# Attention scores: the rounding-remainder pass split into two 64-row matmuls on different keys

## The chip, the cores and the metric

The kernel runs on one NeuronCore of a Trainium2 chip. The metric is the device time of one execution in microseconds (us). TensorE (PE) multiplies, VectorE (DVE), ScalarE (ACT) and GpSimd (POOL) do the elementwise work, SyncE (SP) and others issue the transfers. A change is called faster or slower when it moves the time by more than 0.3%, 7.9 us here.

## The reference, cut to what matters

Two layers of a diffusion backbone. The part that is touched is the differential attention of the first layer: six heads, each with two sets of queries and keys of 64 channels and one set of values of 128 channels; 1024 latent tokens ask, 256 context tokens and the 1024 latent tokens answer.

```python
s = jnp.einsum('bqhcd,bkhcd->bchqk', qi, k) * scale      # c = 0, 1: two score maps per head
p = jax.nn.softmax(s, axis=-1)
wgt = p[:, 0] - lam * p[:, 1]
return jnp.einsum('bhqk,bkhe->bqhe', wgt, v)
```

## The kernel before, in words

Everything is computed in fp32. A matmul operand is kept as two rounded parts, high and low (fp32r), and a product of two operands is the sum of products of the parts. `spill_q` and `spill_k` (L661 to L673) leave the queries and keys of each head in DRAM, transposed, with both parts: `qt_d[h, c, part, 64 channels, token]` and `kt_d[h, c, copy, 64 channels, part, key]`, where the two copies of the keys are equal.

`head_load` (L840) brings one head into SBUF. The tile `q` has on its 128 partitions the high part of the 64 channels and below it the low part; the tile `k` has the same 64 channels of the keys on both halves, once with the high and once with the low part. So a matmul over 128 rows gives (query high + query low) times one part of the keys, and `s_mm` (L856) makes the scores of 128 queries against 1280 keys in six matmuls: three stretches of keys (512, 512, 256 columns, one PSUM bank each), each with the high and then the low part of the keys.

`attention` (L780) walks over 48 tiles of 128 queries (6 heads of 8 tiles), software pipelined. Its order is written by hand and pinned on PE, ACT, DVE and POOL: each of these engines works through its instructions in the order of the program. In one step s the order is

- PE: `s_mm` for c=0; transposes `wT` group 0 of tile s-2; `s_mm` for c=1; (every second step two transposes of `pair_out`); 4 matmuls of `pv`; `wT` group 1; 6 matmuls of `pv`; `wT` group 2.
- DVE: `combine` of tile s-1 (a reciprocal and a scalar product, L883 and L884, which need the row sums of the exponential for c=1 of the last step); the two row maxima for c=0 (L867); their minimum after negation (L871); (a copy of `pair_out`, L928); the two maxima for c=1; an operation of the head's tail (`tail_op`, L938 to L950) if there is one; the minimum for c=1 (L871); the copy L909 of `wT` group 2.
- ACT: the copy L907 of `wT` group 0; the exponential for c=0 (L877); (two squares of `pair_out`, L931); the copy L907 of group 1; the exponential for c=1.
- POOL: the two operations of `combine` of tile s-1, L889 (scale) and L890 (add), on 128x1280 elements; then what `head_load` issues, one part per step.

The score tile `s` has two buffers of three PSUM banks, one for c=0 and one for c=1, so `s_mm` for c waits until the exponential for c of the last step has read them. The tile of the transposes, `tr`, has one buffer: `wT` group 1 waits for the copy of what stands there before, group 2 for the copy L907 of group 1.

`head_load` of head h+1 runs during head h: a transfer for `q` in the second step, for `k` (c=0 and c=1) in the third and fourth, all three issued by POOL, and one for `v` issued by SP in the fifth. The transfers of the first head are issued in the stage before.

Of the kernel before, what the change touches and what calls it, by code (L numbers as in the profile page):

```python
# [10 lines left out]
F32R = mybir.dt.float32r  # L11
# [6 lines left out]
P = 128  # L18
D = 1024
SEQ = 1024  # L20
CTX = 256
NK = SEQ + CTX
# [4 lines left out]
NT = SEQ // P  # L27
# [19 lines left out]
class Net:  # L47
# [791 lines left out]

    def head_load(self, h, hp, hd):  # L840
        nc = self.nc
        qs = hp.tile([P, 2, SEQ], F32R, tag="q", name=self.name("q"))
        ks = hp.tile([P, 2, 2, NK], F32R, tag="k", name=self.name("k"))
        v = hp.tile([P, NK], F32, tag="v", name=self.name("v"))
        hd[h] = {"q": qs, "k": ks, "v": v, "o": self.xt([P, NT, P]),
                 "z0": self.small([P, NT], "z0", 2), "ms": self.small([P, NT], "ms", 2)}
        yield
        nc.gpsimd.dma_start(out=qs, in_=self.qt_d[h].rearrange("c a p t -> (a p) c t"))
        yield
        for c in range(2):  # L850
            nc.gpsimd.dma_start(out=ks[:, c], in_=self.kt_d[h, c].rearrange("d p a t -> (d p) a t"))
            yield
        nc.sync.dma_start(out=v, in_=self.v_d[h])
        yield

    def s_mm(self, st, c):  # L856
        nc, hd, t = self.nc, st["h"], st["t"]
        st["s"][c] = s = self.sp.tile([P, NK], F32, tag="s", name=self.name("sc"))
        for o0, n in ((0, 512), (512, 512), (1024, 256)):
            for a in range(2):  # L860
                nc.tensor.matmul(s[:, o0:o0 + n], hd["q"][:, c, t * P:(t + 1) * P], hd["k"][:, c, a, o0:o0 + n],  # L861
                                 start=(a == 0), stop=(a == 1))
        st["nm"][c] = self.small([P, 2], "nm")

    def s_max(self, st, c, i):
# [827 lines left out]
```

## Time and profile before

| | |
|---|---|
| time before, median of 3 runs | 2635.67 us (2633.87 to 2640.92) |
| the profiled execution: time | 2635.35 us |
| the profiled execution: span from first to last instruction | 2633.6 us |
| mean granted TensorE clock | 0.989 of full |
| PE busy | 2539.0 us (96%) |
| DVE busy | 1849.5 us (70%) |
| ACT busy | 1255.7 us (48%) |
| POOL busy | 949.5 us (36%) |
| score matmuls (L861) | 576, first start 341.2 us, last 654.2 us |

Busy is the sum of the durations that the profile shows for an engine, as a share of the span. Matmuls are pipelined: the next one starts before the end that is shown for the last. The score matmuls mark the attention stage, some 313 us of the span.

### The profile page before, as it was taken

The page shows a single profiled execution, that of the slowest core. Times are in us where ns is not written, and L with a number is a line of the kernel's source. Part 1 is how long each engine was busy: PE and PEld are TensorE (multiplying, and loading weights), DVE is VectorE, ACT ScalarE, POOL GpSimd, SP SyncE. Part 2 cuts the span into 40 slices and gives each one's busy share as a digit, 9 for nine tenths or more (in the row PEclk, how much of TensorE's full clock was granted, in tenths as well). Part 3 has the DMA queues.
Part 4 walks back from the last instruction along what each step waited for, and adds up shares of the span by engine and source line. Part 5 has one row for each costly group of instructions (what it writes and reads, how often), then busy time and mean ns, then how long its engine had stood idle before and what let it go on. Part 6 is the DMA issues. An engine that isn't in the chain of part 4 may idle for free. (4 is left out here: it accounts for less than half of the span.)

```text
span 2633.6 us, 33489 instructions
## 1 busy us (share of the span) xinstructions
PE 2539.0 (96%) x12251; PEld 2111.1 (80%) x12251; DVE 1849.5 (70%) x2862; ACT 1255.7 (48%) x2363; POOL 949.5 (36%) x582
## 2 busy tenths in 40 slices
PE   6999989999988999999999999999999999999999
PEld 5999977777777888888888877888888788888887
DVE  4777678888777555579877665666788655668884
ACT  5332356666343333358775323553654333338780
POOL 5432356666013223125461211230424232205452
PEclk8999999999999999999999999999999999999999
DMA  9577532320532333543303375447123333463302
GB/s 272 178 235 238 188 118 67 103 95 1 212 133 83 107 117 110 186 169 127 128 33 132 121 255 176 136 136 267 66 98 102 105 112 112 136 248 128 114 28 91
DMA packets 206290, 359.84 MB, mean 137 GB/s; under 512 B 16455, under 2 KB 110490, under 8 KB 201006
## 3 DMA queue, kind: packets, MB, share of 16 engines
q1 hardware_dynamic: 180816, 270.10, 31.5%
q0 software_dynamic: 10144, 47.19, 5.3%
q10 hardware_dynamic: 15166, 40.42, 4.0%
q8 instruction: 96, 1.57, 0.2%
q14 instruction: 68, 0.56, 0.1%
HBM read 264.56 MB, written 93.10 MB: 136 GB/s over the span
## 5 line engine op out<-in xcount | busy, mean ns | idle before, releaser
L105 DVE TENSOR_TENSOR w<-s,w 128x512 fp32r<-128x512 f32 (+3 forms) x311 | 291.6, 954 | 199.7 <-ACT w L104 196.9
L130 PE MATMUL ps<-w,hid 128*128 128x512 f32 x928 | 362.4, 390 | 2.4 <-DVE x L1347 2.3
L132 PE MATMUL ps<-w,hid 128*128 128x512 f32 x928 | 361.1, 389 | 0.0
L131 PE MATMUL ps<-w,hid 128*128 128x512 f32 x928 | 361.1, 389 | 0.0
L104 ACT CAST w<-s 128x512 fp32r<-128x512 f32 (+2 forms) x313 | 212.9, 693 | 296.6 <-POOL s L1151 76.7
L112 ACT CAST tr<-h 128x512 fp32r<-128x512 f32 x392 | 220.7, 587 | 109.1 <-DVE w L113 50.5
L1285 POOL TENSOR_TENSOR h<-h,h 128x2048 f32<-128x2048 f32 x36 | 170.6, 4743 | 141.1 <-DVE h L1253 92.5
L1151 POOL TENSOR_TENSOR s<-s,s 128x512 f32<-128x512 f32 x36 | 48.3, 1343 | 440.2 <-DVE w L105 440.2
L130 PEld LDWEIGHTS ps<-w,hid 128*128 128x128 f32 x928 | 174.2, 188 | 40.3 <-issue 2.8
L132 PEld LDWEIGHTS ps<-w,hid 128*128 128x128 f32 x928 | 174.2, 188 | 36.1
L131 PEld LDWEIGHTS ps<-w,hid 128*128 128x128 f32 x928 | 174.2, 188 | 35.6
L877 ACT ACTIVATE e<-sc,nm 128x1280 f32<-128x1280 f32 x96 | 127.6, 1329 | 106.6 <-DVE nm L871 104.9
L113 DVE TENSOR_TENSOR hid<-h,tr 128x512 fp32r<-128x512 f32 x196 | 132.0, 685 | 54.3 <-ACT tr L112 51.2
L1288 POOL TENSOR_TENSOR h<-h,h 128x2048 f32<-128x2048 f32 x14 | 70.7, 5053 | 264.6 <-DVE h L1285 264.6
L130 PE MATMUL ps<-h,w 128*128 128x512 f32 x416 | 165.0, 397 | 0.1
L131 PE MATMUL ps<-h,w 128*128 128x512 f32 x416 | 162.8, 391 | 1.4 <-DVE h L296 1.4
L132 PE MATMUL ps<-h,w 128*128 128x512 f32 x416 | 163.0, 392 | 0.0
L861 PE MATMUL sc<-k,q 128*128 128x512 f32 (+1 forms) x576 | 139.9, 380 | 14.0 <-ACT e L877 12.2
L867 DVE TENSOR_REDUCE nm<-sc 128x1 f32<-128x768 f32 x192 | 148.6, 816 | 0.4 <-PE sc L861 0.4
L890 POOL TENSOR_TENSOR e<-e,e 128x1280 f32<-128x1280 f32 x47 | 136.3, 2901 | 3.9
L861 PEld LDWEIGHTS sc<-k,q 128*128 128x128 f32 x576 | 103.7, 193 | 40.7 <-ACT e L877 20.1
L114 ACT CAST hid<-h 128x512 fp32r<-128x512 f32 x196 | 119.4, 623 | 23.7 <-PE ps L131 15.5
(325 smaller groups left out, 6600.0 us busy)
## 6 DMA issues: line engine op xcount, KB each, us to landing
s<-in_ffn_w_dram SPq DMA_DIRECT2D x80, 512.0 KB
hid_d<-h SPq DMA_DIRECT2D x28, 1024.0 KB
h<-hid_d SPq DMA_DIRECT2D x56, 512.0 KB
ad<-in_ada_w_dram SPq DMA_DIRECT2D x48, 512.0 KB
h<-in_ffn_w_dram SPq DMA_DIRECT2D x24, 1024.0 KB
s<-in_od_w_in_dram SPq DMA_DIRECT2D x32, 512.0 KB
ad<-in_ada_w_dram POOLq DMA_DIRECT2D x32, 512.0 KB, 5.4
k<-kt_d POOLq DMA_DIRECT2D x12, 1280.0 KB, 7.8
```

The costliest lines, as they stand in the source:

```text
L104: nc.scalar.copy(out=hi, in_=src)
L105: nc.vector.tensor_sub(lo, src, hi.bitcast(F32))
L112: nc.scalar.copy(out=r.bitcast(F32R), in_=x)
L113: nc.vector.tensor_sub(l, x, r)
L130: nc.tensor.matmul(ps, ah, bh, start=first, stop=False, skip_group_check=more)
L131: nc.tensor.matmul(ps, ah, bl, start=False, stop=False, skip_group_check=more)
L132: nc.tensor.matmul(ps, al, bh, start=False, stop=last, skip_group_check=more)
L861: nc.tensor.matmul(s[:, o0:o0 + n], hd["q"][:, c, t * P:(t + 1) * P], hd["k"][:, c, a, o0:o0 + n], start=(a == 0), stop=(a == 1))
L867: self.nc.vector.tensor_reduce(st["nm"][c][:, i:i + 1], st["s"][c][:, s], axis=AX.X, op=ALU.max, negate=True)
L877: nc.scalar.activation(e, st["s"][c], AF.Exp, bias=nm[:, 0:1], accum_out=z)
L890: nc.gpsimd.tensor_add(e0, e0, e1)
L1285: return lambda: eng.tensor_sub(raw[o], raw[x], raw[y])
```

## The change

`head_load` lays the tiles out differently and `s_mm` uses them so:

- The keys' high part keeps its two copies on 128 rows. Of the low part there is one copy now, in the columns from NK on (`lo`): rows 0 to 63 hold the keys 0 to 511 and, behind them, 1024 to 1279; rows 64 to 127 hold the keys 512 to 1023.
- The queries' high part is needed on both halves of the rows. For c=0 the tile `q` has it on rows 0 to 63, for c=1 (the halves are swapped) on rows 64 to 127; a new tile `q2` has the copy on the other rows. `qa` is the high part on rows 0 to 63, `qb` that on rows 64 to 127.
- `s_mm` still has six matmuls. Three over 128 rows with the keys' high part; three over 64 rows with the keys' low part: `qa` against the keys 0 to 511, `qb` against the keys 512 to 1023, `qa` against the last 256. The order is 512, 512 (128 rows), 512, 512 (64 rows), 256 (128 rows), 256 (64 rows).
- The product of the queries' low part and the keys' low part is no longer computed.
- For each head POOL issues 13 transfers in place of 3, in four steps (2, 3, 4, 4); that of `v` comes one step later.

```diff
     def head_load(self, h, hp, hd):
         nc = self.nc
+        eng = nc.gpsimd
         qs = hp.tile([P, 2, SEQ], F32R, tag="q", name=self.name("q"))
-        ks = hp.tile([P, 2, 2, NK], F32R, tag="k", name=self.name("k"))
+        ks = hp.tile([P, 2, NK + 768], F32R, tag="k", name=self.name("k"))
         v = hp.tile([P, NK], F32, tag="v", name=self.name("v"))
-        hd[h] = {"q": qs, "k": ks, "v": v, "o": self.xt([P, NT, P]),
+        q2 = hp.tile([P, SEQ], F32R, tag="q2", name=self.name("q"))
+        hd[h] = {"q": qs, "k": ks, "v": v, "qa": (qs[0:64, 0], q2[0:64]), "qb": (q2[64:P], qs[64:P, 1]), "o": self.xt([P, NT, P]),
                  "z0": self.small([P, NT], "z0", 2), "ms": self.small([P, NT], "ms", 2)}
         yield
-        nc.gpsimd.dma_start(out=qs, in_=self.qt_d[h].rearrange("c a p t -> (a p) c t"))
+        eng.dma_start(out=qs[:, 0], in_=self.qt_d[h, 0].rearrange("a p t -> (a p) t"))
+        eng.dma_start(out=q2[64:P], in_=self.qt_d[h, 0, 0])
+        yield
+        for a in range(2):
+            eng.dma_start(out=qs[64 - 64 * a:P - 64 * a, 1], in_=self.qt_d[h, 1, a])
+        eng.dma_start(out=q2[0:64], in_=self.qt_d[h, 1, 0])
         yield
         for c in range(2):
-            nc.gpsimd.dma_start(out=ks[:, c], in_=self.kt_d[h, c].rearrange("d p a t -> (d p) a t"))
+            lo = ks[:, c, NK:]
+            eng.dma_start(out=ks[:, c, 0:NK], in_=self.kt_d[h, c, :, :, 0].rearrange("d p t -> (d p) t"))
+            eng.dma_start(out=lo[0:64, 0:512], in_=self.kt_d[h, c, 0, :, 1, 0:512])
+            eng.dma_start(out=lo[64:P, 0:512], in_=self.kt_d[h, c, 1, :, 1, 512:1024])
+            eng.dma_start(out=lo[0:64, 512:768], in_=self.kt_d[h, c, 0, :, 1, 1024:NK])
             yield
         nc.sync.dma_start(out=v, in_=self.v_d[h])
         yield
@@ def s_mm(self, st, c):
-        for o0, n in ((0, 512), (512, 512), (1024, 256)):
-            for a in range(2):
-                nc.tensor.matmul(s[:, o0:o0 + n], hd["q"][:, c, t * P:(t + 1) * P], hd["k"][:, c, a, o0:o0 + n],
-                                 start=(a == 0), stop=(a == 1))
+        w = slice(t * P, (t + 1) * P)
+        k, lo = hd["k"][:, c, 0:NK], hd["k"][:, c, NK:]
+        for o in (slice(0, 512), slice(512, 1024)):
+            nc.tensor.matmul(s[:, o], hd["q"][:, c, w], k[:, o], start=True, stop=False)
+        nc.tensor.matmul(s[:, 0:512], hd["qa"][c][:, w], lo[0:64, 0:512], start=False, stop=True)
+        nc.tensor.matmul(s[:, 512:1024], hd["qb"][c][:, w], lo[64:P, 0:512], start=False, stop=True)
+        nc.tensor.matmul(s[:, 1024:NK], hd["q"][:, c, w], k[:, 1024:NK], start=True, stop=False)
+        nc.tensor.matmul(s[:, 1024:NK], hd["qa"][c][:, w], lo[0:64, 512:768], start=False, stop=True)
```

## Rows read from the trace of the kernel before

**Rows 1.** Busy us (count) of PE, PEld, DVE, ACT, POOL in attention; clock; DMA share; GB/s.

```profile
458.00:510.00 52.00, 49.16 (x260) 38.36 (x259) 42.92 (x87) 33.50 (x71) 34.92 (x20) 1.00 0.26 84
```

**Rows 2.** Timeline of DVE, ACT and POOL: start, duration, instruction, idle before.

```profile
490.18 2.90 POOL L890 TENSOR_TENSOR e<-e,e 128x1280 f32<-128x1280 f32 x1
...
491.60 0.30 ACT L931 ACTIVATE oT<-x 128x128 f32<-128x128 f32 x1
...
492.07 1.03 DVE L871 TENSOR_TENSOR nm<-nm 128x1 f32<-128x1 f32 x1
...
492.18 0.57 ACT L907 COPY pt<-tr 128x512 f32<-128x512 f32 x1
...
493.20 1.33 ACT L877 ACTIVATE e<-sc,nm 128x1280 f32<-128x1280 f32 x1 [0.34 <-DVE ms L943]
...
494.98 1.55 DVE L867 TENSOR_REDUCE nm<-sc 128x1 f32<-128x768 f32 x2
495.24 1.34 POOL L889 TENSOR_SCALAR e<-e,cc 128x1280 f32<-128x1280 f32 x1 [2.15 <-DVE cc L884]
...
496.57 0.16 DVE L871 TENSOR_TENSOR nm<-nm 128x1 f32<-128x1 f32 x1
...
496.66 2.91 POOL L890 TENSOR_TENSOR e<-e,e 128x1280 f32<-128x1280 f32 x1
```

**Rows 3.** Timeline of PE in the same stretch, neighbours of one kind merged.

```profile
489.45 0.38 PE L927 MATMUL tr<-ident,oT 128*128 128x128 f32 x2
489.67 1.03 PE L916 MATMUL pv<-pt,v 128*128 128x256 f32 x4
...
492.80 0.44 PE L903 MATMUL tr<-ident,e 128*128 128x128 f32 x2 [0.22 <-ACT pt L907]
492.99 1.41 PE L861 MATMUL sc<-k,q 128*128 128x512 f32 x6
...
494.24 0.60 PE L903 MATMUL tr<-ident,e 128*128 128x128 f32 x4
...
494.67 1.42 PE L861 MATMUL sc<-k,q 128*128 128x512 f32 x6
...
495.93 1.03 PE L916 MATMUL pv<-pt,v 128*128 128x256 f32 x4
...
496.79 0.60 PE L903 MATMUL tr<-ident,e 128*128 128x128 f32 x4
497.23 1.46 PE L916 MATMUL pv<-pt,v 128*128 128x256 f32 x6
```

**Rows 4.** Timeline of PE where four matmuls on 32-column tiles interrupt 128x128 ones.

```profile
712.17 0.39 PE L131 MATMUL ps<-w,m 128*128 128x512 f32 x1
712.40 0.39 PE L132 MATMUL ps<-w,m 128*128 128x512 f32 x1
712.72 1.05 PE L172 MATMUL tr<-s,one 128*32 128x512 f32 x4
713.70 0.50 PE L130 MATMUL ps<-w,m 128*128 128x512 f32 x1
714.04 0.39 PE L131 MATMUL ps<-w,m 128*128 128x512 f32 x1
```

**Rows 5.** Timeline of PE around a transpose over 32 rows.

```profile
1620.36 1.03 PE L1568 MATMUL tr<-ident,s 128*128 128x128 f32 x8
1621.32 0.24 PE L1571 MATMUL tr<-ident,s 32*128 32x32 f32 x1
1621.49 0.50 PE L130 MATMUL ps<-h,w 128*128 128x512 f32 x1
```

**Rows 6.** The 256-column score matmuls: count, busy, mean ns, idle before.

```profile
L861 PE MATMUL sc<-k,q 128*128 128x256 f32 x152 | 30.1, 279 | 0.0
```

**Rows 7.** POOL's transfer issues in the attention stage: line, count, busy, mean ns.

```profile
L851 POOL DMA_DIRECT2D k<-kt_d x10 | 6.0, 602 | 0.0
L848 POOL DMA_DIRECT2D q<-qt_d x5 | 3.9, 777 | 0.0
```

## The prediction, made before the changed kernel ran

> **What bounds the kernel now.** I read the page first, then the busy times of the attention stage, then the timeline there. The busy times [rows 1] make PE look like the bound: 49.16 of 52 us. That is misleading, because a matmul's shown end lies behind the start of the next. The timeline tells what PE really needs. From start to start [rows 3], a step takes 0.19 us for the last two transposes (492.80 to 492.99), 1.25 for the scores of c=0, 0.43 for four transposes, 1.26 for the scores of c=1, 0.86 for four pv matmuls, 0.44 for four transposes, and at the pace of the four 6 x 0.215 = 1.29 for six more: 5.72 us, and in every second step 0.22 more for pair_out (489.45 to 489.67). The mean is 5.83 us.
>
> The step takes longer, and the other engines say why [rows 2]. POOL's L890 ends at 493.08 (490.18 + 2.90) and the next one at 499.57 (496.66 + 2.91): 6.49 us. The chain between them holds no PE. The minimum for c=1 (L871), an operation that takes 0.16 us alone, began at 492.07 inside L890 and ended at 493.10, just behind L890's end: DVE's operation on SBUF was held until POOL's was through. Then the exponential (0.10 later, 1.33 long), the row sum, the reciprocal and L884 (L889 starts 0.71 after the exponential's main part), L889 to L890 (1.42), and L890 (2.91). 0.12 + 1.33 + 0.71 + 1.42 + 2.91 = 6.49. PE has 0.66 us to spare per step.
>
> Two margins matter. The maxima for c=0 start at 494.98, 0.58 us after the last score matmul's shown end (492.99 + 1.41 = 494.40). And the minimum for c=0 starts at 496.57, only 0.09 us ahead of L890 (496.66): it slips in before POOL takes hold.
>
> **The scores' matmuls, step by step.** What a change between full and partial tiles of the array costs is read where it occurs already [rows 4, 5]. Ordinary 512-column matmuls follow each other at 0.23 us. Ahead of the 32-column tiles the next one starts 0.32 us after, that is 0.07 before the shown end of the last (712.40 + 0.39 = 712.79, start 712.72). The same 0.07 holds on the way back (712.72 + 1.05 = 713.77, start 713.70), into the 32-row transpose (1621.39, 1621.32) and out of it (1621.56, 1621.49). So the array is emptied at each switch. The first matmul behind it is also 0.11 us longer (0.50, not 0.39), since its weights aren't loaded under the last one; its successor starts 0.34 later, not 0.23. The four tile matmuls also show that tiles run abreast: each streams 512 fp32 columns, which at pv's 0.215 us for 256 would be 1.72 us in a row, and all four were through in 1.05.
>
> The new order in `s_mm` has four switches: before `qa`, before the 256-column matmul, before the last `qa`, and behind it. Against before:
> - second 512-column matmul: 0.32 for 0.23, +0.09;
> - `qa` and `qb` abreast: 0.50 - 0.07 = 0.43 for two passes of 0.23, -0.03;
> - the two 256-column matmuls: 0.28 shown [rows 6] + 0.11 - 0.07 = 0.32 each, for half of 0.23 each, +0.41;
> - weights of whatever comes next: between 0 and 0.11; nothing tells which, so I take the middle, 0.05.
>
> Together +0.52 us per `s_mm`, 1.04 per step: PE needs 5.83 + 1.04 = 6.87 us. The scores become visible later by 0.09 - 0.03 + 0.20 + 0.11 = 0.37 us: 1.78 after the first matmul's start, not 1.41. If `qa` and `qb` run one after the other, a further 0.23 is lost: 7.33 us per step. If there is no emptying between 64 and 128 rows, each `s_mm` is 0.23 shorter.
>
> No row shows a 64-row tile. The Trainium skill (TensorEngine Tiling (Array Packing), Key Properties) says that changing the tiling mode, not just the tile, drains the engine, and lists 64 rows as a mode of its own; by it all four switches cost what the 32-row one does, and the sum stays. Its Theoretical Speedup for a contraction of 64 rows, up to two times, would leave only the saving; that is the third rival below.
>
> **Where the delay goes.** 6.87 is more than 6.49, so PE falls behind the other engines by 0.38 us a step. The slack of 0.58 - 0.37 = 0.21 ahead of the maxima is gone after one step. From then on the maxima for c=0 start late, while `combine`, ahead of them on DVE, doesn't, and POOL's L890 comes on time. As soon as the maxima are over 0.09 late, their minimum begins inside L890 and is held to its end, as the minimum for c=1 is now. Behind it on DVE stand the copy L928 and the maxima for c=1; behind the exponential for c=0 on ACT stand the squares, the copy L907 that PE's last transposes wait for, and the exponential for c=1.
>
> The step is then, from L890's end to the next: 0.12 to the exponential for c=0, 1.33; in every second step the squares, 0.58 (491.60 to 492.18); L907, 0.57; the exponential for c=1, 1.33 (its minimum is ready before: 0.02 + 1.55 + about 0.2); then 0.71 + 1.42 + 2.91 [rows 2]. That is 8.39 or 8.97, 8.68 in the mean: 2.19 more than 6.49.
>
> Does this state hold itself up? Count from L907's end. PE: 0.05 and 0.19 to the scores (492.75, 492.80, 492.99), 1.78 until they are visible, 1.59 for the maxima (494.98 to 496.57): the minimum comes at 3.61. POOL: 1.33 + 0.71 + 1.42: L890 starts at 3.46. The minimum is 0.15 late and is held again. With the 1.41 of before it would come at 3.24, 0.22 early: the kernel of before falls out of this state, the changed one stays in it. The switch lies at 0.22 us of delay in the scores; I expect 0.37.
>
> **The transfers.** Ten more issues per head at 0.60 to 0.78 us [rows 7], up to four in a step: 2.4 to 3.1 us on POOL behind L890. Today POOL idles 2.15 us there [rows 2], in an 8.68 us step 4.3: they cost nothing. If the step stays at 6.49 that cover is too small, and two steps of each of five heads lose 0.25 to 0.95 us, 3 to 10 us in all. The data have three steps to land and are hidden either way, as is the transfer for v a step later; the PE waits on more semaphores once per head only.
>
> **The sum.** pv fills PE's step from the fifth step on: 44 steps x 2.19 = 96 us; the four steps ahead of it, limited by the first pass through the pipeline, about 1. Profiled time 2635.35 (span 2633.6 and 1.7 around it, as good as the median of 2635.67) + 97 = 2732 us.
>
> **Rivals.**
> 1. The array is emptied, but the minimum for c=0 is never held, or in some steps only. PE alone sets the step: 0.38 x 44 = 17 us, 2652; with `qa` and `qb` in a row 0.84 x 44 = 37, 2673; held in half of the steps, some 2690. For it: the margins that decide, 0.09 and 0.15 us, are small. Against it: a held minimum puts the scores so late that the next is held too.
> 2. `qa` and `qb` in a row and the minimum held: 7.33 is still under 8.68, so the time is the forecast's.
> 3. Emptying is not needed between 64 and 128 rows. Each `s_mm` is shorter, but the 6.49 us chain holds no PE, so nothing is won but some 2 us in the first steps, and POOL's issues cost 3 to 10: 2636 to 2644, about 2639, no slower than can be told. It decides if the four switches together cost under the 0.66 us that PE has to spare per step. Speaking for it: only 32-row and 32-column tiles were seen. Against: all four switches seen cost the same.
> 4. With more empty time on PE its clock, 1.00 in the stage [rows 1], falls to 1.2 GHz for long. Doubling the streamed part of PE's 6.87 us makes it some 11: 4.5 x 44, above 2800.
>
> **Chances.** Forecast, with rival 2: 0.58, 2715 to 2755 (held from the second step on: 47 x 2.19 gives 2739). Rival 1: 0.24, 2648 to 2714. Rival 3: 0.11. Faster for a reason I don't see: 0.03. Above 2760, the clock among others: 0.04. The range 2648 to 2760 leaves out rival 3 and the two last, 0.18. Under 0.3% (7.9 us) a measurement can't tell from no change: faster 0.04, same 0.10, slower 0.86.
>
> **What the changed profile would show.** 64-row score matmuls whose starts lie 0.07 before the shown end of the full ones; the pair starting within some 0.01 us; the 256-column ones of 0.39, not 0.28. Minima L871 for c=0 of up to 3 us that end with L890, in nearly every step; 8.4 and 9.0 us from L890 to L890; PE waiting for L907 and L928. Minima of 0.16 throughout would refute the held state, and 256-column matmuls at the old pace the emptying. It is wrong most easily in the 0.15 us by which the state holds itself up.

## The result and the profile after

The changed kernel takes 2729.35 us (median of 4, 2724.77 to 2732.49), the one before 2636.86 (median of 4 beside it, 2633.87 to 2640.92): a ratio of 1.0348, 95% interval 1.0327 to 1.0369. The profiled execution took 2732.49 us with a span of 2730.7, 97.1 more than the span before.

First the busy time of each engine in a stretch of the attention stage (columns as in [rows 1]):

```profile
341.00:381.00 40.00, 34.91 (x111) 20.28 (x109) 25.77 (x51) 18.24 (x30) 24.08 (x21) 0.63 0.57 155
...
537.00:589.00 52.00, 42.42 (x198) 27.16 (x198) 43.23 (x68) 25.78 (x53) 31.01 (x23) 1.00 0.26 63
```

In 52 us PE is busy for 42.4 where it was for 49.2, ACT for 25.8 where it was for 33.5, POOL for 31.0 where it was for 34.9 [rows 1]. Only DVE is as busy as before, and its figure contains the time for which its operations are held. So no engine became the bound; the engines wait for each other longer. The first line shows that PE's clock was low at the stage's start (0.63 in the mean; 0.87 in the same stretch of the kernel before).

The timeline of DVE, ACT and POOL over one step, which answers to [rows 2]. The lines of the file have moved: L882 is the maximum, L886 the minimum, L892 the exponential, L922 the copy of the transposes, L904 and L905 are POOL's two operations.

```profile
542.10 1.56 DVE L882 TENSOR_REDUCE nm<-sc 128x1 f32<-128x768 f32 x2 [0.18 <-PE sc L877]
...
543.50 2.90 POOL L905 TENSOR_TENSOR e<-e,e 128x1280 f32<-128x1280 f32 x1
543.69 2.72 DVE L886 TENSOR_TENSOR nm<-nm 128x1 f32<-128x1 f32 x1
...
546.44 1.33 ACT L892 ACTIVATE e<-sc,nm 128x1280 f32<-128x1280 f32 x1 [3.18 <-DVE nm L886]
...
547.76 0.58 ACT L922 COPY pt<-tr 128x512 f32<-128x512 f32 x1
...
548.23 1.34 ACT L892 ACTIVATE e<-sc,nm 128x1280 f32<-128x1280 f32 x1
...
550.28 1.35 POOL L904 TENSOR_SCALAR e<-e,cc 128x1280 f32<-128x1280 f32 x1 [3.89 <-DVE cc L899]
...
551.71 2.89 POOL L905 TENSOR_TENSOR e<-e,e 128x1280 f32<-128x1280 f32 x1
...
551.99 2.62 DVE L886 TENSOR_TENSOR nm<-nm 128x1 f32<-128x1 f32 x1
```

The maxima of c=0 now wait for PE (0.18 us, "PE sc L877"); before, 0.58 us lay between the scores and them [rows 2, 3]. Their minimum starts 0.19 us after POOL's addition, and an operation that took 0.16 us takes 2.72: it ends at 546.41, with the addition (546.40). ACT waits 3.18 us for it. From there the chain runs without another gap: exponential, copy, exponential of c=1, then 0.71 us to L904, and L905 ends at 554.60, 8.20 us after the last one. There the next minimum is already held.

PE in the same stretch, from the last transposes of a step on (it answers to [rows 3]; the 64-row matmuls are L874, L875 and L877):

```profile
548.39 0.44 PE L918 MATMUL tr<-ident,e 128*128 128x128 f32 x2 [1.43 <-ACT pt L922]
548.59 0.71 PE L873 MATMUL sc<-k,q 128*128 128x512 f32 x2
...
549.23 0.49 PE L874 MATMUL sc<-k,q 64*128 64x512 f32 x1
549.23 0.50 PE L875 MATMUL sc<-k,q 64*128 64x512 f32 x1
...
549.66 0.39 PE L876 MATMUL sc<-k,q 128*128 128x256 f32 x1
...
549.98 0.38 PE L877 MATMUL sc<-k,q 64*128 64x256 f32 x1
...
550.29 0.66 PE L918 MATMUL tr<-ident,e 128*128 128x128 f32 x4
```

4.5 us earlier, behind the scores of c=1, where the pv matmuls come next:

```profile
544.10 1.13 PE L931 MATMUL pv<-pt,v 128*128 128x256 f32 x4
...
545.06 0.60 PE L918 MATMUL tr<-ident,e 128*128 128x128 f32 x4
```

The two 64-row matmuls start at the same hundredth of a us, so they do run abreast. The first starts 0.07 us before the shown end of the full ones (548.59 + 0.71 = 549.30), and so does each one behind a switch: by the reading of [rows 4, 5] the array is emptied between 64 and 128 rows too. The 256-column matmuls are shown with 0.38 and 0.39 us, not 0.28 [rows 6]. From the first start to the next transposes `s_mm` takes 1.70 us (1.25 before), and the scores are visible after 1.77 (549.98 + 0.38 - 548.59; 1.41 before).

POOL's L905 ran 47 times, first at 356.7 and last at 748.1 us; its counterpart before first at 353.1 and last at 655.0. So 3.6 of the 97.1 us of span lie ahead of the first, 89.5 between the first and the last (391.5 for 302.0), and 4.0 behind. The ends of successive L905 are 6.46 and 7.08 us apart in the first two steps, then 8.70 and 10.49, and from there on 8.2 and 8.8 in turn, with a few longer ones, 8.54 in the mean, to the last step. Before it was 6.56 (302.0 us for the 46 steps).

### The profile page after: what moved, and what is told of

Same layout as the page of the kernel before. It is cut to its first block, busy times and chain, and to the rows that moved or that the text cites. A ratio compares the mean times of both kernels' runs of the same rounds, so it can differ in the third digit from the quotient of the medians.

```text
span 2730.7 us, 33566 instructions
## 1 busy us (share of the span) xinstructions
PE 2592.7 (95%) x12251; PEld 2101.3 (77%) x12251; DVE 1914.4 (70%) x2862; ACT 1253.3 (46%) x2363; POOL 980.4 (36%) x642
## 5 line engine op out<-in xcount | busy, mean ns | idle before, releaser
L892 ACT ACTIVATE e<-sc,nm 128x1280 f32<-128x1280 f32 x96 | 127.8, 1331 | 142.4 <-DVE nm L886 142.2
L882 DVE TENSOR_REDUCE nm<-sc 128x1 f32<-128x768 f32 x192 | 148.7, 815 | 17.4 <-PE sc L877 17.0
L918 PE MATMUL tr<-ident,e 128*128 128x128 f32 x460 | 83.0, 297 | 61.7 <-ACT pt L922 34.9
L905 POOL TENSOR_TENSOR e<-e,e 128x1280 f32<-128x1280 f32 x47 | 135.9, 2892 | 3.9
L918 PEld LDWEIGHTS tr<-ident,e 128*128 128x128 f32 x460 | 52.5, 146 | 97.1 <-ACT pt L922 52.5
```

The lines of the kernel that those rows point to most:

```text
L882: self.nc.vector.tensor_reduce(st["nm"][c][:, i:i + 1], st["s"][c][:, s], axis=AX.X, op=ALU.max, negate=True)
L892: nc.scalar.activation(e, st["s"][c], AF.Exp, bias=nm[:, 0:1], accum_out=z)
L905: nc.gpsimd.tensor_add(e0, e0, e1)
L918: nc.tensor.transpose(out=ps[:, j, :], in_=st["e"][0][:, k * P:(k + 1) * P], identity=self.ident)
```

## The experiments

Four kernels ran on one chip, four on another, each beside the kernel before: its medians were 2633.17 us on the first and 2635.89 on the second.

**Two switches, not four.** The changed kernel with the full matmul on the last 256 keys moved ahead of the 64-row ones:

```diff
         for o in (slice(0, 512), slice(512, 1024)):
             nc.tensor.matmul(s[:, o], hd["q"][:, c, w], k[:, o], start=True, stop=False)
+        nc.tensor.matmul(s[:, 1024:NK], hd["q"][:, c, w], k[:, 1024:NK], start=True, stop=False)
         nc.tensor.matmul(s[:, 0:512], hd["qa"][c][:, w], lo[0:64, 0:512], start=False, stop=True)
         nc.tensor.matmul(s[:, 512:1024], hd["qb"][c][:, w], lo[64:P, 0:512], start=False, stop=True)
-        nc.tensor.matmul(s[:, 1024:NK], hd["q"][:, c, w], k[:, 1024:NK], start=True, stop=False)
```

> The changed kernel with its score matmuls in another order: the three over 128 rows first, then the three over 64 rows, so two switches between full and 64-row tiles per score map and not four. Held-minimum theory: the scores are visible after 0.31 + 0.23 + 0.21 (256 columns ahead of a switch) + 0.34 + 0.28 = 1.37 us, no later than the 1.41 of the kernel before; PE needs some 6.0 us per step, under the 6.49 of the other engines; no minimum for c=0 is held, and only the transfers' 3 to 10 us are left: 2636 to 2647 us. Rival, every switch costs its own time on a PE that sets the step: half of the loss stays, about 2683. Rival, the transfers or the layout cost the time: 2729, as the changed kernel.

Measured: 2638.53 us, ratio 1.0020 (1.0002 to 1.0037). The rival with half of the loss (2683) is out, and so is the one that puts the loss down to transfers and layout. The timeline of PE:

```profile
485.93 0.70 PE L873 MATMUL sc<-k,q 128*128 128x512 f32 x2
486.48 0.28 PE L874 MATMUL sc<-k,q 128*128 128x256 f32 x1
486.69 0.50 PE L875 MATMUL sc<-k,q 64*128 64x512 f32 x1
486.69 0.50 PE L876 MATMUL sc<-k,q 64*128 64x512 f32 x1
487.02 0.27 PE L877 MATMUL sc<-k,q 64*128 64x256 f32 x1
487.23 0.66 PE L918 MATMUL tr<-ident,e 128*128 128x128 f32 x4
```

The scores are visible after 1.36 us (1.37 in the expectation), and the attention stage runs at the old pace: POOL's 47 additions end between 361.96 and 664.19 us, 302.2 us as against 302.0 before. The 5 us that the time is longer lie outside of this stretch; the first addition ends 6.0 us later than before, and the first score matmul starts 6.0 later (347.23 for 341.22). Part of the delay shows in the stage before, in which POOL issues the transfers of the first head (POOL, then PE):

```profile
321.55 0.51 POOL L862 DMA_DIRECT2D k<-kt_d  x1 [0.65 <-DMA q<-qt_d]
322.07 1.44 POOL L600 TENSOR_TENSOR m<-qn,x 128x256 f32<-128x256 f32 x2
```

```profile
328.74 0.33 PE L613 MATMUL tr<-ident,m 128*128 128x128 f32 x1 [2.32 <-POOL m L607]
```

The last of the thirteen issues ends at 322.06 (before, the last of three at 309.76), POOL's own work follows only then, and PE waits 2.32 us for POOL. The changed kernel has such a wait of 2.27 us, the kernel before none, and thirteen transfers in the old layout (below) one of 0.22. 1.75 us of the 6.0 lie ahead of these transfers (the first is issued at 308.35 for 306.60). No run tested this delay by itself.

**Nothing for POOL to hold.** The changed kernel, all its matmuls and transfers, with one maximum over 1280 keys for c=0:

```diff
         s = (slice(0, 512), slice(512, NK))[i]
+        if c in (0,):
+            if i == 1:
+                return
+            s = slice(0, NK)
         self.nc.vector.tensor_reduce(st["nm"][c][:, i:i + 1], st["s"][c][:, s], axis=AX.X, op=ALU.max, negate=True)
...
-        nc.vector.tensor_tensor(nm[:, 0:1], nm[:, 0:1], nm[:, 1:2], op=ALU.min)
+        if c not in (0,):
+            nc.vector.tensor_tensor(nm[:, 0:1], nm[:, 0:1], nm[:, 1:2], op=ALU.min)
```

> The changed kernel with one maximum over all 1280 keys for c=0 in place of two and their minimum; all matmuls and transfers stay. Held-minimum theory: nothing is left for c=0 that POOL could hold, so PE alone sets the step, 6.9 us: 2645 to 2665 us, and the period of the step 6.8 to 7.0. Rival, the four switches cost their time directly: the matmuls are the same, so 2720 to 2729.

Measured: 2649.43 us, ratio 1.0068 (1.0048 to 1.0089): of the 3.5% of the change 0.7% are left, with the four switches in place. POOL's timeline gives the period (L910 is the addition here):

```profile
502.13 2.90 POOL L910 TENSOR_TENSOR e<-e,e 128x1280 f32<-128x1280 f32 x1
...
509.03 2.90 POOL L910 TENSOR_TENSOR e<-e,e 128x1280 f32<-128x1280 f32 x1
...
515.58 2.90 POOL L910 TENSOR_TENSOR e<-e,e 128x1280 f32<-128x1280 f32 x1
```

6.90 and 6.55 us in turn, 6.73 in the mean, a little under the 6.8 to 7.0 that was expected. The first four steps are longer here too (32.2 us in all, 25.8 in the kernel before).

**The transfers alone.** The kernel before with thirteen transfers per head:

```diff
+        eng = nc.gpsimd
...
-        nc.gpsimd.dma_start(out=qs, in_=self.qt_d[h].rearrange("c a p t -> (a p) c t"))
+        for a in range(2):
+            eng.dma_start(out=qs[64 * a:64 * a + 64, 0], in_=self.qt_d[h, 0, a])
+        yield
+        eng.dma_start(out=qs[0:64, 1], in_=self.qt_d[h, 1, 0])
+        for t in range(2):
+            eng.dma_start(out=qs[64:P, 1, t * 512:t * 512 + 512], in_=self.qt_d[h, 1, 1, :, t * 512:t * 512 + 512])
         yield
         for c in range(2):
-            nc.gpsimd.dma_start(out=ks[:, c], in_=self.kt_d[h, c].rearrange("d p a t -> (d p) a t"))
+            eng.dma_start(out=ks[:, c, 0], in_=self.kt_d[h, c, :, :, 0].rearrange("d p t -> (d p) t"))
+            for o0, n in ((0, 512), (512, 512), (1024, 256)):
+                eng.dma_start(out=ks[:, c, 1, o0:o0 + n], in_=self.kt_d[h, c, :, :, 1, o0:o0 + n].rearrange("d p t -> (d p) t"))
             yield
```

> The kernel before with its queries and keys brought in by thirteen transfers per head from POOL, in four steps of 2, 3, 4 and 4 as in the changed kernel; layout and matmuls are those of before. Held-minimum theory: POOL idles 2.15 us per step and four issues take 2.2 to 2.4, so at most 1 us in two steps per head: 2636 to 2647 us. Rival, the transfers cost the time: about 2729.

Measured: 2633.43 us, ratio 0.9999 (0.9987 to 1.0011). In the old layout the thirteen transfers cost nothing.

**A delay without any 64-row tile.** The kernel before with two more full matmuls per score map, whose result the next ones write over:

```diff
+        for o0 in (0, 512):
+            nc.tensor.matmul(s[:, o0:o0 + 512], hd["q"][:, c, t * P:(t + 1) * P], hd["k"][:, c, 0, o0:o0 + 512],
+                             start=True, stop=True)
         for o0, n in ((0, 512), (512, 512), (1024, 256)):
```

> The kernel before with two additional 512-column matmuls over 128 rows at the start of each score map (their result is written over by the next ones); no 64-row tile, no switch, transfers as before. Held-minimum theory: the scores are visible 0.46 us later and PE needs 6.75 us per step, so the minimum for c=0 falls under L890 and stays there: steps of 8.2 and 8.8 us, about 2725 us, as with the change. Rival, PE's time alone counts: 0.26 x 44 = 11 us, about 2648.

Measured: 2719.58 us, ratio 1.0340 (1.0317 to 1.0363): the loss of the change, from matmuls of the ordinary kind. The groups of DVE by line show the minimum in three kernels between 400 and 640 us, each in its own fence: first the changed kernel, then two switches, then this one.

```profile
L886 DVE TENSOR_TENSOR nm<-nm 128x1 f32<-128x1 f32 x57 | 81.0, 1420 | 1.4
```

```profile
L886 DVE TENSOR_TENSOR nm<-nm 128x1 f32<-128x1 f32 x73 | 24.7, 338 | 1.7
```

```profile
L874 DVE TENSOR_TENSOR nm<-nm 128x1 f32<-128x1 f32 x56 | 76.5, 1365 | 1.3
```

A mean of 1.4 us is that of one minimum of 2.5 to 2.7 and one of 0.16 in each step. Here the ends of POOL's additions are 6.5 us apart for eight steps, and from the ninth on 8.2 and 8.8; by the sum PE falls back by 0.26 us per step and so uses up its slack in the first ones, which was not followed step by step.

**Half of that delay.** One additional matmul per map, `for o0 in (0,):` in the diff above.

> The kernel before with one additional 512-column matmul over 128 rows at the start of each score map. PE needs 6.29 us, under 6.49, and the scores come 0.23 us later, under the 0.55 of slack ahead of the maxima. Held-minimum theory: no step is entered late, the time stays, 2633 to 2642 us, unless the slow steps of the beginning put it into the held state, which at 0.23 us would be just able to go on (then towards 2700). Rival, each matmul more costs its time: 0.46 us x 48, about 2655.

Measured: eleven executions took 2630.81, 2632.43, 2632.77, 2634.63, 2637.28, 2639.24, 2651.69, 2658.58, 2719.37, 2721.07 and 2721.62 us; these are the times of one program. Without the three longest the ratio is 1.0007 (0.9984 to 1.0031). Here the split itself is the result: at 0.23 us of delay both rhythms occur, and an execution ends in the one or the other. The profile caught one of 2719.37 us, and its timelines of PE, DVE and POOL show the entry, and a later step.

```profile
369.85 0.58 PE L860 MATMUL sc<-k,q 128*128 128x512 f32 x1
370.22 2.34 PE L864 MATMUL sc<-k,q 128*128 128x512 f32 x6
...
404.92 2.33 PE L864 MATMUL sc<-k,q 128*128 128x512 f32 x6
```

```profile
372.59 1.55 DVE L870 TENSOR_REDUCE nm<-sc 128x1 f32<-128x768 f32 x2 [0.18 <-PE sc L864]
374.18 2.75 DVE L874 TENSOR_TENSOR nm<-nm 128x1 f32<-128x1 f32 x1
...
382.37 2.75 DVE L874 TENSOR_TENSOR nm<-nm 128x1 f32<-128x1 f32 x1
...
408.88 1.45 DVE L874 TENSOR_TENSOR nm<-nm 128x1 f32<-128x1 f32 x1
```

```profile
374.01 2.91 POOL L893 TENSOR_TENSOR e<-e,e 128x1280 f32<-128x1280 f32 x1
...
382.22 2.88 POOL L893 TENSOR_TENSOR e<-e,e 128x1280 f32<-128x1280 f32 x1
...
407.38 2.93 POOL L893 TENSOR_TENSOR e<-e,e 128x1280 f32<-128x1280 f32 x1
```

One group of six score matmuls took 2.34 us where its neighbours take 1.32, with PE's clock low (0.63 from 369 to 373 us). The maxima waited 0.18 us, their minimum came 0.17 after POOL's addition, and was held to 376.93. The kernel before has a group of 2.17 us at that place too (370.67) and keeps its rhythm. The clock was back at 1.00 from 376 us on, and the next three minima, with no slow group in between, were 0.14 to 0.15 too late again. From 404.92 on such a slow group came back in every second step, there the minimum was 1.1 to 1.5 us too late, and the clock was 0.90 in the mean. So this trace shows the held rhythm at full clock for four steps only; the execution of 2721.07 us had a mean clock of 0.989, that of the kernel before, so it can't have had many slow groups. It was not profiled, and neither were the two of some 2655; that those left the rhythm half-way is a guess.

**No minimum at all.** The edit of the second experiment for both maps (`(0, 1)` in place of `(0,)`), in the kernel before, in the changed one, and in that with two switches.

> The kernel before with one maximum over all 1280 keys in place of two and their minimum, for c=0 and c=1. Held-minimum theory: the 6.49 us chain is gone with the minimum for c=1 that closed it, and PE's own 5.83 us (5.9 to 6.0 with small waits) sets the step: 0.5 to 0.6 us less in 44 steps, 2605 to 2618 us. Rival, the chain of 6.49 us is set by POOL's and ACT's own work and not by the held minimum: no change, about 2633.

> The changed kernel with one maximum over all 1280 keys for c=0 and c=1. With nothing left to hold, PE sets the step here and in the like version of the kernel before, and the difference of the two is what the four switches cost PE: by the sum 0.52 us per score map, 1.04 per step, some 44 to 50 us between the two, so 2650 to 2665 us. Rival, the pair on 64 rows earns its own cost: no more than 10 us between the two.

> The changed kernel with the three full matmuls first and the three over 64 rows behind them, and one maximum for c=0 and c=1. By the sum two switches and one 512-column pass less come to 0.07 to 0.13 us per score map more than before, 0.2 per step: 6 to 12 us above the like version of the kernel before, 2612 to 2628 us. Rival, two switches cost half of what four do: 22 to 25 us above it.

Measured: the kernel before with it takes 2591.93 us, ratio 0.9834 (0.9817 to 0.9851), faster than both kernels; the changed one 2646.71, ratio 1.0051 (1.0032 to 1.0069); with two switches 2604.44, ratio 0.9883 (0.9865 to 0.9902). All three are faster than expected. POOL's additions in the kernel before and then in the changed one:

```profile
506.14 2.90 POOL L895 TENSOR_TENSOR e<-e,e 128x1280 f32<-128x1280 f32 x1
...
512.23 2.91 POOL L895 TENSOR_TENSOR e<-e,e 128x1280 f32<-128x1280 f32 x1
...
517.54 2.90 POOL L895 TENSOR_TENSOR e<-e,e 128x1280 f32<-128x1280 f32 x1
```

```profile
505.97 2.90 POOL L910 TENSOR_TENSOR e<-e,e 128x1280 f32<-128x1280 f32 x1
...
512.49 2.91 POOL L910 TENSOR_TENSOR e<-e,e 128x1280 f32<-128x1280 f32 x1
...
519.45 2.91 POOL L910 TENSOR_TENSOR e<-e,e 128x1280 f32<-128x1280 f32 x1
```

Two steps take 11.40 us in the first and 13.48 in the second: with nothing held for c=0 and c=1, the new matmuls cost PE 1.04 us in each of these steps. Over the last 42 steps it is 1.01 us each, 42.5 in all; the first four cost 10.3 more (the changed kernel has steps of up to 10.86 us there). The times differ by 55 us, a little over the 44 to 50 expected. Two switches cost 12.5 us, against the 6 to 12 expected, and 0.20 us in each of the last 42 steps, as expected.

What PE does between the two score maps, and ahead of them, in the kernel before and then in the changed one:

```profile
503.29 0.38 PE L908 MATMUL tr<-ident,e 128*128 128x128 f32 x2
503.43 1.40 PE L861 MATMUL sc<-k,q 128*128 128x512 f32 x6
504.67 0.60 PE L908 MATMUL tr<-ident,e 128*128 128x128 f32 x4
505.02 1.42 PE L861 MATMUL sc<-k,q 128*128 128x512 f32 x6
```

```profile
504.83 0.66 PE L923 MATMUL tr<-ident,e 128*128 128x128 f32 x4
505.25 0.71 PE L873 MATMUL sc<-k,q 128*128 128x512 f32 x2
```

## Why the prediction was right

**What bounds the kernel.** Right, and shown by the one maximum in the kernel before. If POOL's and ACT's own work had set 6.49 us, it would have changed nothing; it took 44 us off. What closed that chain is not always the minimum for c=1, though: it is held under L890 in 20 of the 47 steps. In the other 27 an operation of the head's tail, which stands ahead of it on DVE, is held, and the minimum comes behind it, as in the step after the one of [rows 2]:

```profile
498.11 1.48 DVE L944 TENSOR_TENSOR ms<-ms,rr 128x8 f32<-128x8 f32 x1
```

**PE's own step.** 0.13 us too long in the sum: without minima it takes 5.70 us, not 5.83. The rows of the kernel before held waits: four transposes take 0.35 us (504.67 to 505.02), not 0.43, and the last two 0.14 (503.29 to 503.43), not 0.19. With the change it is 6.74, not 6.87, so the difference of 1.04 came out.

**The price of the switches.** 64 rows count as a mode of their own, and each of the four switches emptied the array. Term by term: the two full 512-column matmuls 0.64 (548.59 to 549.23), which leaves 0.33 for the second if the first takes the 0.31 that was expected of it (0.32 in the sum); the pair 0.43 of 0.43; the 256-column ones 0.32 and 0.31 of 0.32; visible scores 1.77 of 1.78. By this `s_mm` itself takes 0.45 us more (1.70 for 1.25). The weights of the next operation come on top, 0.05 in the sum: behind c=1 four pv matmuls take 0.96 us (544.10 to 545.06) for 0.86 [rows 3], and behind c=0 four transposes 0.42 (504.83 to 505.25) for 0.35. The Trainium skill (TensorEngine Tiling (Array Packing), Key Properties) says that a change of mode drains the engine and that tiles work independently; the trace agrees with both.

**Where the delay goes.** Right. Minima of 2.1 to 2.8 us that end with POOL's addition stand in every step from 390 us on; the first one for c=0 is held at 371.53, in the fourth step and not the fifth, while the clock is low. With the delay and without the tiles (extra2) the loss is there, without the minimum (onemax0) most of it is gone. That onemax0's 2649 us is so near the first rival's 2652 is partly luck: its last 42 steps lose 0.17 us each against the kernel before, 7 us and not 17, and its first four steps 6. The Trainium skill (SBUF — State Buffer, Who interferes with whom) says that a DVE instruction with two SBUF inputs contends with a GpSimd one that reads SBUF, and that the lock on the ports which they share is exclusive. The trace agrees: 2.72 us for 0.16, ended 0.01 us after POOL's.

**That the state holds itself up.** Right that it does; where its edge lies was not measured. In the step shown, POOL's addition starts 3.37 us after the copy's end (548.34), not 3.46, and the minimum 3.65 after it, not 3.61: 0.28 too late, not 0.15. Other steps have less to spare: about one in eight of the changed kernel some 0.15 us, and with 0.23 us of delay (extra1) one in eight 0.03 to 0.06. By these tightest steps the edge lies at some 0.2 us, an estimate. That is near the forecast 0.22, which came from another step with other sizes, so the agreement is partly luck, and no run had a delay between 0 and 0.23. At 0.23 the program goes either way; at 0.36 and 0.46 none of four executions each stayed out.

**The size.** The forecast of 2732 us for a measured 2729.35 is better than its terms. 44 steps of 2.19 us were forecast, 96 us. Between POOL's first and last addition there are 46 steps, and the last 42 of them take 8.54 us, not 8.68, and before 6.57, not 6.49: 83 us, some 14 less. In the held step of 8.20 the exponential for c=0 starts 0.04 us after the addition's end, not 0.12, and the exponential for c=1 0.11 before the shown end of the copy ahead of it (548.23, 548.34). As much was missing: the first four steps cost 6.9 us and not 1 (one at a granted clock of 0.81 took 10.49), the attention stage began 3.6 us later, and 4.0 us were lost behind it. That the two cancel is luck.

**The transfers.** Free within the attention stage, as forecast; also at the old step length, where 3 to 10 us had been allowed for and none was measured. Not counted in the forecast were the thirteen of the first head in the stage before. There PE waits 2.27 us for POOL, which could be most of the 3.6; no run tested it by itself.

**The rivals.** The first (PE alone) is what is left when the hold is taken away. The third fell with the first 64-row start. The fourth came in a small form only: the clock was 0.63 in the mean from 341 to 381 us (0.87 before) and 1.00 in the stretch shown from 537 on.

## What to carry to other kernels

A 64-row pair beside 128-row matmuls saves one pass and pays for a switch in and a switch out; group everything of one tile shape, or the switches eat the gain (with no minimum in the way four cost 55 us here, two 12.5; the pair never won). And look at margins, not only at busy shares: a short VectorE operation with two SBUF inputs that slips in 0.09 us ahead of a long GpSimd one is a cliff: 0.46 us more of matmuls per step can cost nothing or 2 us per step. Taking that operation out, for both maps, took 44 us off the kernel before; no form of the pair took anything off.

## What the hardware showed that I had not expected

One maximum over 1280 score columns in three PSUM banks took 1.49 us alone, against 1.55 for two and 0.16 for their minimum, so leaving out the minimum costs nothing. The line is that of the kernel before without a minimum, between 400 and 600 us:

```profile
L871 DVE TENSOR_REDUCE nm<-sc 128x1 f32<-128x1280 f32 x70 | 104.2, 1488 | 6.9 <-PE sc L861 4.5
```

One program ran in two rhythms, 86 us apart; in the one execution that was profiled, the longer rhythm began with one slow group of six matmuls at 370 us. And PE's clock was lower at the stage's start in the changed kernel (0.63 from 341 to 381 us, 0.87 before), where the PE waits for the first passes.
